# A two-stream hybrid layer on one NeuronCore: the pivots and the last range's statistics in PSUM banks

## Chip, core and metric

The kernel runs on one core of a Trainium2 chip. The metric is the device time of one execution in microseconds (us). The four engines that compute are TensorE (PE; PEld is its weight load), VectorE (DVE), ScalarE (ACT) and GpSimd (POOL). SyncE (SP) issues DMAs. SBUF is the memory that all engines read; TensorE writes its products to banks of PSUM, which VectorE and ScalarE read and write too.

## The reference

One layer of a hybrid encoder is computed for a prompt (1024 frames) and for running streams (32 frames), 1056 columns in all, with the same weights. What matters here are the two residual sublayers at its end, each with a layer norm over the 1024 features:

```python
mix = jnp.concatenate([hm, hf, hg], axis=-1) @ w_o
x = _layer_norm(ALPHA * x + (1 + g1) * mix, ln1_g, ln1_b)
h = x * (1 + sc2) + sh2
y = (jax.nn.silu(h @ w_gate) * (h @ w_up)) @ w_down
x = _layer_norm(ALPHA * x + (1 + g2) * y, ln2_g, ln2_b)
# _layer_norm: mu = mean(x); var = mean((x - mu)^2); (x - mu) * rsqrt(var + eps) * g + b
```

## The kernel before

**Layout.** Features lie on the 128 partitions in eight blocks (`k` or `m`, 0 to 7), frames along the free axis. The frames are two parts, c=0 (512) and c=1 (544), and each is worked in two ranges (256 and 256, 272 and 272; `MM` and `LN`). A large product takes three matmuls per block: the operand and the weight are split into a high and a low part, and hi·hi, hi·lo and lo·hi are added (`gemm`, L131 to L133; the names end in `whi`/`wlo`, `ah`/`al`, `acth`/`actl`). Weights come by DMA, ScalarE casts the high part (L118) and VectorE subtracts for the low one (L119).

**Order of stages.** Projections, the head groups, then `wo0`: the output projection and first layer norm (`lna0`) of c=0. After that heads of the other part, the SwiGLU products of c=0 (`up0`, `dn0`) interleaved with what is left of the attention heads, then `wo1`, `lna1`, `up1`, `dn1` for c=1 with the second layer norm (`lnb`). A tile scheduler fixes each engine's order ahead of the run from a cost model; `issue_after` keeps what follows behind a named instruction, and pools with a fixed number of buffers make a new tile wait for the release of an old one. PSUM has three pools in the late stages: `pg` (3 banks, `"g"`), `pu` (3 banks, `"gu"`) and `pt` (2 banks, `"t"`); while the attention runs `pss` (2 banks, `"s"`) stands in place of `pu`.

**A residual update.** `sublayer_end` (L1185 on) adds one finished block from its PSUM bank to the residual tile `z` on VectorE (L1195, `scalar_tensor_tensor`, STT below). The bank is free for the next product when this is done. So VectorE's queue up to L1195 decides when TensorE may begin the product that reuses the bank.

**The pivot.** To keep the sums of squares small, the column mean of the first finished block is taken off all eight blocks (`ln_pivot`, L1049). A matmul with a matrix of ones (L1052) forms it in a `"t"` bank, ScalarE copies it to SBUF (`pv`, L1053), VectorE subtracts it from the first block (L1054), and GpSimd from each other block (L1189) before that block's L1195.

**The sums.** `ln_sum` squares a block on ScalarE (L1063) into an SBUF tile `tmp` (4 buffers); GpSimd or VectorE adds blocks up to `zs` (L1067, GpSimd in `wo1` and `dn1`) and VectorE the squares to `qs` (L1069). In the last range of all, the last two blocks aren't added but go to the matmul with ones beside `zs` and `qs` (`late`, `rest`, L1079).

**The closing norm.** `ln2` (L1436) forms mean and mean square by matmul, copies the mean to SBUF (L1445), forms the variance (L1446), Ln and Exp on ScalarE, a Newton step on VectorE (L1088 to L1090), then per block: minus mean (L1448, VectorE), times 1/std (L1464, VectorE), gain and offset (L1466 on ScalarE, L1468 on VectorE for the last block), and a store per two blocks, the last two singly (L1471). c=1 does range 272 first (`half` 0), whose norm is woven into the second range's products; range 0 (`half` 1) ends the kernel.

## Time and profile before

| | us |
|---|---|
| median of three timed runs | 1342.64 (1341.70 to 1343.36) |
| the profiled execution's own time | 1339.63 |
| its span in the trace | 1337.8 |
| TensorE busy in the span | 1320.8 (99%) |
| VectorE / ScalarE / GpSimd busy | 990.1 / 651.2 / 212.9 |

A row of the timeline gives the start in us, the duration, the engine, the line, the operation, output<-inputs, shapes and types, and how many instructions in a row were put together (x3); in brackets the idle time of that engine just before, and what ended it. A row of the waits gives an engine and line, what it waited for, the total in us, how often, and the longest. A row of the windows gives, for a stretch, each engine's busy time and instructions, the granted TensorE clock, the DMA share and GB/s. The lines named below are those of the kernel before.

### The profile page before, as it was taken

The numbers are of one execution on the slowest core, as the hardware profiler recorded it, in microseconds if no ns is written. First come the engines' busy times: TensorE is split into PE (matmuls) and PEld (weight loads), VectorE is DVE, ScalarE is ACT, GpSimd is POOL, SyncE is SP. The second block draws the span as 40 slices with busy tenths as digits, with TensorE's granted clock in tenths as the row PEclk, the third lists the DMA queues.
The fourth block names the chain that finished last, engine by engine and source line by source line (L and its number), as shares of the span: only waits on it lengthen the run. The fifth ranks groups of instructions, "written<-read, shape, count | busy, mean of one in ns | idle before, by whom it ended". The sixth has DMA issues, their size and how long they took to land.

```text
span 1337.8 us, 24992 instructions
## 1 busy us (share of the span) xinstructions
PE 1320.8 (99%) x9428; PEld 1198.5 (90%) x9428; DVE 990.1 (74%) x2081; ACT 651.2 (49%) x1291; POOL 212.9 (16%) x242
## 2 busy tenths in 40 slices
...
GB/s 362 280 257 168 174 180 183 148 129 110 234 178 249 172 156 113 132 153 127 118 130 116 88 119 80 228 153 113 208 236 148 227 198 165 195 121 150 87 48 67
DMA packets 118120, 217.43 MB, mean 163 GB/s; under 512 B 18325, under 2 KB 62481, under 8 KB 118001
## 3 DMA queue, kind: packets, MB, share of 16 engines
...
q8 instruction: 74, 1.21, 0.4%
q10 hardware_dynamic: 1200, 0.62, 0.2%
...
## 4 chain that ended last, share of the span: by engine, by line
PE 95%; DVE 2%; DMA 2%; ACT 1%; issue 0%; SPq 0%; DVEq 0%
PE up_g L131 6%; PE up_g L133 6%; PE up_g L132 6%; PE dn_g L131 4%; PE dn_g L132 4%; PE dn_g L133 4%; PE tm_g L405 3%; PE tm_g L407 3%; PE tm_g L406 3%; PE sup_u L133 3%; PE sup_u L132 3%; PE sup_u L131 3%; PE fox_t L939 2%; PE wo_g L131 2%; PE wo_g L133 2%; PE wo_g L132 2%
## 5 line engine op out<-in xcount | busy, mean ns | idle before, releaser
L131 PE MATMUL up_g<-ada_ah,up_whi 128*128 128x512 f32 (+1 forms) x384 | 140.8, 367 | 0.0
L132 PE MATMUL up_g<-ada_al,up_whi 128*128 128x512 f32 (+1 forms) x384 | 140.7, 366 | 0.0
L133 PE MATMUL up_g<-ada_ah,up_wlo 128*128 128x512 f32 (+1 forms) x384 | 139.7, 364 | 0.0
L1364 ACT CAST sup_whi<-sup_raw 128x1024 fp32r<-128x1024 f32 x54 | 56.6, 1050 | 97.6 <-PE dn_u L132 41.3
L912 ACT ACTIVATE fox_p<-fox_s,fox_fmx 128x384 f32<-128x384 f32 (+2 forms) x96 | 55.1, 578 | 59.4 <-DVE fox_fmx L910 39.8
L131 PEld LDWEIGHTS up_g<-ada_ah,up_whi 128*128 128x128 f32 x384 | 72.5, 189 | 11.7 <-issue 0.4
L133 PEld LDWEIGHTS up_g<-ada_ah,up_wlo 128*128 128x128 f32 x384 | 72.6, 189 | 11.2
L132 PEld LDWEIGHTS up_g<-ada_al,up_whi 128*128 128x128 f32 x384 | 72.6, 189 | 10.6
L1365 DVE TENSOR_TENSOR sup_wlo<-sup_raw,sup_whi 128x1024 fp32r<-128x1024 f32 x54 | 69.0, 1279 | 15.1 <-ACT sup_whi L1364 15.1
L1195 DVE SCALAR_TENSOR_TENSOR wo_z<-dn_g,start_mod,wo_z 128x512 f32<-128x512 f32 (+4 forms) x120 | 60.1, 520 | 21.7 <-PE dn_g L133 21.1
L118 ACT CAST up_whi<-up_raw 128x1024 fp32r<-128x1024 f32 x50 | 52.4, 1049 | 47.4 <-PE dn_g L132 19.0
L132 PE MATMUL dn_g<-up_actl,dn_whi 128*128 128x512 f32 (+2 forms) x200 | 73.2, 367 | 0.0
L133 PE MATMUL dn_g<-up_acth,dn_wlo 128*128 128x512 f32 (+2 forms) x200 | 73.2, 366 | 0.0
L131 PE MATMUL dn_g<-up_acth,dn_whi 128*128 128x512 f32 (+2 forms) x200 | 73.1, 366 | 0.0
L119 DVE TENSOR_TENSOR up_wlo<-up_raw,up_whi 128x1024 fp32r<-128x1024 f32 x50 | 63.6, 1272 | 11.3 <-ACT up_whi L118 10.2
L944 ACT CAST fox_pth<-fox_t 128x512 fp32r<-128x512 f32 (+1 forms) x80 | 41.3, 542 | 51.6 <-PE fox_t L939 45.5
L907 DVE TENSOR_REDUCE fox_fmx<-fox_s 128x1 f32<-128x384 f32 (+2 forms) x96 | 53.0, 553 | 15.5 <-PE fox_s L904 14.1
L118 ACT CAST dn_whi<-dn_raw 128x1024 fp32r<-128x1024 f32 (+1 forms) x44 | 42.7, 970 | 43.3 <-PE up_g L132 26.8
L945 DVE TENSOR_TENSOR fox_ptl<-fox_t,fox_pth 128x512 fp32r<-128x512 f32 (+1 forms) x80 | 49.8, 632 | 9.8 <-ACT fox_pth L944 9.6
L119 DVE TENSOR_TENSOR dn_wlo<-dn_raw,dn_whi 128x1024 fp32r<-128x1024 f32 (+1 forms) x44 | 49.5, 1125 | 8.0 <-ACT dn_whi L118 8.0
L1316 POOL DMA_DIRECT2D start_dp<-w_gu x19 | 20.2, 1063 | 212.8 <-DMA start_dp<-w_gu 212.8
L405 PE MATMUL tm_g<-tm_whi,start_ah 128*128 128x264 f32 (+2 forms) x160 | 49.9, 312 | 0.0
...
## 6 DMA issues: line engine op xcount, KB each, us to landing
...
```

The source lines that it names most:

```text
L118: nc.scalar.copy(hi[:, :w], raw[:, :w])
L119: (eng or nc.vector).tensor_tensor(lo[:, :w], raw[:, :w], f(hi[:, :w]), ALU.subtract)
L131: nc.tensor.matmul(ps, hi, xh(k), start=start and k == 0, stop=False)
L132: nc.tensor.matmul(ps, hi, xl(k), start=False, stop=False)
L133: self.lastmm = nc.tensor.matmul(ps, lo, xh(k), start=False, stop=stop and k == n - 1)
L405: nc.tensor.matmul(ps[:, :ncol], xh, hi, start=k == 0, stop=False)
L907: nc.vector.tensor_reduce(mxs[:, x:x + 1], s[:, :w], AX.X, ALU.max, negate=True)
L912: nc.scalar.activation(pr[:, lo:hi], banks[x][:, :hi - lo], AF.Exp, bias=mxs[:, 0:1], accum_out=sums[:, x:x + 1])
L945: nc.vector.tensor_tensor(pl[:, :e], ps[:, :e], f(ph[:, :e]), ALU.subtract)
L1195: self.lastz = self.nc.vector.scalar_tensor_tensor(z[:, m, x:y], ps[:, x - a:y - a], g[i], z[:, m, x:y], ALU.mult, ALU.add)
L1364: nc.scalar.copy(h, x)
L1365: tt(l, x, f(h), ALU.subtract)
```

## The change

Four things are done; c=1's other stages and all matmuls of the products are the same.

1. Where sums are taken (`wo0`, `wo1`), the pivot stays in its PSUM bank. ScalarE's copy goes. VectorE takes the pivot off every block with an STT that reads the bank (`ln_off`, L1061 of the changed kernel), eight times per range; GpSimd's 28 subtractions (L1189) go. In `wo0` the bank is from `pss`, in `wo1` from `pt`.
2. `ln2_half` (c=1, first range): mean and 1/std stay in `pt` banks and VectorE reads them there.
3. `ln_sum` in the last range: squares go to `pg`/`pu` banks (the last one to SBUF), and the addition of a square to `qs` is issued behind the update of the block after it.
4. `ln2_last` (c=1, second range): mean, variance and 1/std in banks; VectorE subtracts the mean from blocks 0 to 2 and GpSimd, from an SBUF copy, from 3 to 7; then VectorE multiplies all eight; blocks 5 and 7 get gain and offset on VectorE, the others on ScalarE. Only the seventh and eighth block's sums and the eighth's square go to the matmul with ones directly.

```diff
     def ln_pivot(self, st, z, sl):
         nc = self.nc
-        ps = self.t(self.pt, [P, 512], F32, "t")
         n = sl.stop - sl.start
+        pool, tag = st["bank"]
+        ps = self.t(pool, [P, 512], F32, tag)
         nc.tensor.matmul(ps[:, :n], self.onesm, z[:, sl], start=True, stop=True)
+        if st["sum"]:
+            st["off"][sl.start] = ps[:, :n]
+            self.ln_off(st, z, sl)
+            return
         nc.scalar.activation(st["pv"][:, sl], ps[:, :n], AF.Copy, scale=float(D // P))
         nc.vector.tensor_tensor(z[:, sl], z[:, sl], st["pv"][:, sl], ALU.subtract)
+
+    def ln_off(self, st, z, sl):
+        self.nc.vector.scalar_tensor_tensor(z[:, sl], st["off"][sl.start], -float(D // P), z[:, sl], ALU.mult, ALU.add)
...
-        sq = self.t(self.p2, [P, 272], F32, "tmp", 4)[:, :sl.stop - sl.start]
+        if st["last"] and m != o[7]:
+            sq = self.t((self.pg, self.pu)[m % 2], [P, 512], F32, self.utag[m % 2])[:, :sl.stop - sl.start]
+        else:
+            sq = self.t(self.p2, [P, 272], F32, "tmp", 4)[:, :sl.stop - sl.start]
         nc.scalar.activation(sq, z[:, m, sl], AF.Square)
+        add = lambda: nc.vector.tensor_tensor(st["qs"][:, sl], st["qs"][:, sl], sq, ALU.add)
+        if st["last"]:
+            with self.tc.issue_after(self.lastz.ins):
+                st["last"].pop()()
+            st["last"].append(add if m != o[7] else None)
+            add = lambda: None
...
         if pivot and not first and st["sum"]:
-            less()
+            self.ln_off(st, z[:, m], sl)
...
+    def ln2_last(self, st, a, b):
+        self.phase = "lnb1"
+        nc, z, sl, n = self.nc, self.z[1], slice(a, b), b - a
+        bank = lambda pool, tag: self.t(pool, [P, 512], F32, tag)[:, :n]
+        pm, pq = bank(self.pt, "t"), bank(self.pt, "t")
+        for p, parts in ((pm, [st["zs"][:, sl]] + [x for x, _ in st["rest"]]), (pq, [st["qs"][:, sl], st["rest"][-1][1]])):
+            for i, y in enumerate(parts):
+                nc.tensor.matmul(p, self.onesm, y, start=i == 0, stop=i == len(parts) - 1)
+        v, r = bank(self.pg, "g"), bank(self.pg, "g")
+        s = self.t(self.p2, [P, 272], F32, "tmp", 4)[:, :n]
+        mean, r0 = st["zs"][:, sl], st["pv"][:, sl]
+        nc.scalar.activation(s, pm, AF.Square)
+        nc.scalar.copy(mean, pm)
+        less = lambda k: nc.vector.tensor_tensor(z[:, k, sl], z[:, k, sl], pm, ALU.subtract)
+        for k in range(2):
+            less(k)
+        first = nc.vector.scalar_tensor_tensor(v, pq, self.epsa, s, ALU.add, ALU.subtract)
+        nc.scalar.activation(r0, v, AF.Ln)
+        nc.scalar.activation(r0, r0, AF.Exp, scale=-0.5)
+        with self.tc.issue_after(first.ins):
+            last = less(2)
+        for k in range(3, KT):
+            nc.gpsimd.tensor_tensor(z[:, k, sl], z[:, k, sl], mean, ALU.subtract)
+        with self.tc.issue_after(last.ins):
+            nc.vector.scalar_tensor_tensor(v, v, -0.5, r0, ALU.mult, ALU.mult)
+            nc.vector.tensor_tensor(v, v, r0, ALU.mult)
+            nc.vector.scalar_tensor_tensor(r, v, 1.5, r0, ALU.add, ALU.mult)
+            for k in range(KT):
+                zk = z[:, k, sl]
+                nc.vector.tensor_tensor(zk, zk, r, ALU.mult)
+                self.ln2_end(k, a, b, nc.scalar if k == 6 else nc.sync, k in (5, 7))
...
+        st["bank"] = (self.pss, "s")
...
             if half:
-                st["late"] = st["order"][6:]
+                st["late"], st["last"] = st["order"][6:], [lambda: None]
...
-            end = self.ln2(1, st, a, b, TAFF[half], True)
             if half:
-                weave(end)
+                self.ln2_last(st, a, b)
             else:
+                end = self.ln2_half(st, a, b)
                 next(end)
```

The scheduler moves instructions beyond these lines. On TensorE everything ahead of `wo0` stands as before; from there to `wo1` the order of attention heads, `up0` and `dn0` among each other differs, and after `wo1` it is the same up to the last range. Three places follow, in each the order before and then the changed one.

In the rows of the changed kernel L1212 is the update (L1195 before), L118 the low part (L119), L130 to L132 the products (L131 to L133), L1074 the sum of squares (L1069), L1083 `zs` (L1067).

VectorE in `wo1`, around the first block's updates (`g` are banks with finished products, two ranges per block: 1855 and 1856 are the first block's, 1862 and 1863 the second's, 1869 and 1870 the third's; `t` are the pivots' banks; `wlo` the low parts of weights). Before:

```order
L1054 TENSOR_TENSOR wo1_z1_1851_9897<-wo1_z1_1851_9897,wo1_pv_1850_9896 128x272
L1195 SCALAR_TENSOR_TENSOR wo1_z1_1851_9897<-wo1_g_1856_9906,start_mod_48_152,wo1_z1_1851_9897 128x240
L1195 SCALAR_TENSOR_TENSOR wo1_z1_1851_9897<-wo1_g_1856_9906,start_mod_48_152,wo1_z1_1851_9897 128x32
L1195 SCALAR_TENSOR_TENSOR wo1_z1_1851_9897<-wo1_g_1862_9975,start_mod_48_152,wo1_z1_1851_9897 128x272
L119 TENSOR_TENSOR wo1_wlo_1882_10182<-wo1_raw_1880_10179,wo1_whi_1881_10181 128x1024
L1069 TENSOR_TENSOR wo1_qs_1849_9895<-wo1_qs_1849_9895,wo1_tmp_1864_10003 128x272
L119 TENSOR_TENSOR wo1_wlo_1889_10252<-wo1_raw_1887_10249,wo1_whi_1888_10251 128x1024
L1054 TENSOR_TENSOR wo1_z1_1851_9897<-wo1_z1_1851_9897,wo1_pv_1850_9896 128x272
L1195 SCALAR_TENSOR_TENSOR wo1_z1_1851_9897<-wo1_g_1869_10045,start_mod_48_152,wo1_z1_1851_9897 128x272
L1195 SCALAR_TENSOR_TENSOR wo1_z1_1851_9897<-wo1_g_1863_9976,start_mod_48_152,wo1_z1_1851_9897 128x240
```

Changed:

```order
L1212 SCALAR_TENSOR_TENSOR wo1_z1_1851_9895<-wo1_g_1855_9903,start_mod_48_152,wo1_z1_1851_9895 128x272
L1212 SCALAR_TENSOR_TENSOR wo1_z1_1851_9895<-wo1_g_1856_9904,start_mod_48_152,wo1_z1_1851_9895 128x240
L1212 SCALAR_TENSOR_TENSOR wo1_z1_1851_9895<-wo1_g_1856_9904,start_mod_48_152,wo1_z1_1851_9895 128x32
L118 TENSOR_TENSOR wo1_wlo_1882_10178<-wo1_raw_1880_10175,wo1_whi_1881_10177 128x1024
L1061 SCALAR_TENSOR_TENSOR wo1_z1_1851_9895<-wo1_t_1857_9954,wo1_z1_1851_9895 128x272 x8
L1061 SCALAR_TENSOR_TENSOR wo1_z1_1851_9895<-wo1_t_1858_9960,wo1_z1_1851_9895 128x272 x3
L1212 SCALAR_TENSOR_TENSOR wo1_z1_1851_9895<-wo1_g_1862_9971,start_mod_48_152,wo1_z1_1851_9895 128x272
L1061 SCALAR_TENSOR_TENSOR wo1_z1_1851_9895<-wo1_t_1858_9960,wo1_z1_1851_9895 128x272 x5
L1212 SCALAR_TENSOR_TENSOR wo1_z1_1851_9895<-wo1_g_1863_9972,start_mod_48_152,wo1_z1_1851_9895 128x240
L1212 SCALAR_TENSOR_TENSOR wo1_z1_1851_9895<-wo1_g_1863_9972,start_mod_48_152,wo1_z1_1851_9895 128x32
```

One low-part subtraction (`wlo_1882`) now stands ahead of the pivots, the other (`wlo_1889`) behind the second block's updates, and sixteen subtractions of the pivots stand among them, three of the second range's ahead of the second block's first update.

TensorE in the first block of `wo1` (`ah0`, `al0` are the operand of range 0, `ah272`, `al272` that of range 272, whose last parts are still being made then). Before:

```order
L132 MATMUL wo1_g_1855_9905<-up0_al0_1830_9828,wo1_whi_1853_9901 128x272
L133 MATMUL wo1_g_1855_9905<-up0_ah0_1828_9826,wo1_wlo_1854_9902 128x272
L131 MATMUL wo1_g_1855_9905<-up0_ah0_1828_9826,wo1_whi_1853_9901 128x272
L132 MATMUL wo1_g_1855_9905<-up0_al0_1830_9828,wo1_whi_1853_9901 128x272
L133 MATMUL wo1_g_1855_9905<-up0_ah0_1828_9826,wo1_wlo_1854_9902 128x272
L131 MATMUL wo1_g_1855_9905<-up0_ah0_1828_9826,wo1_whi_1853_9901 128x272
L132 MATMUL wo1_g_1855_9905<-up0_al0_1830_9828,wo1_whi_1853_9901 128x272
L133 MATMUL wo1_g_1855_9905<-up0_ah0_1828_9826,wo1_wlo_1854_9902 128x272
L131 MATMUL wo1_g_1855_9905<-up0_ah0_1828_9826,wo1_whi_1853_9901 128x272
L132 MATMUL wo1_g_1856_9906<-up0_al272_1831_9829,wo1_whi_1853_9901 128x272
```

Changed:

```order
L132 MATMUL wo1_g_1855_9903<-up0_ah0_1828_9824,wo1_wlo_1854_9900 128x272
L130 MATMUL wo1_g_1856_9904<-up0_ah272_1829_9825,wo1_whi_1853_9899 128x272
L131 MATMUL wo1_g_1856_9904<-up0_al272_1831_9827,wo1_whi_1853_9899 128x272
L132 MATMUL wo1_g_1856_9904<-up0_ah272_1829_9825,wo1_wlo_1854_9900 128x272
L130 MATMUL wo1_g_1855_9903<-up0_ah0_1828_9824,wo1_whi_1853_9899 128x272
L131 MATMUL wo1_g_1855_9903<-up0_al0_1830_9826,wo1_whi_1853_9899 128x272
L132 MATMUL wo1_g_1855_9903<-up0_ah0_1828_9824,wo1_wlo_1854_9900 128x272
```

Before, the range 0 products ran ahead, those of range 272 came in as their operand came; changed, the two ranges take turns block by block, three matmuls each.

VectorE at the end of the kernel, from the seventh block's update on (`dn1_u`, `dn1_g` finished products or, in the changed kernel's L1074, squares; `lnb1_t` matmul sums; `sup_pv`, `sup_zs` SBUF copies). Before:

```order
L1195 SCALAR_TENSOR_TENSOR wo1_z1_1851_9897<-dn1_g_2704_15848,start_mod_48_152,wo1_z1_1851_9897 128x272
L1069 TENSOR_TENSOR sup_qs_2570_14857<-sup_qs_2570_14857,dn1_tmp_2701_15819 128x272
L1069 TENSOR_TENSOR sup_qs_2570_14857<-sup_qs_2570_14857,dn1_tmp_2703_15840 128x272
L1195 SCALAR_TENSOR_TENSOR wo1_z1_1851_9897<-dn1_u_2706_15868,start_mod_48_152,wo1_z1_1851_9897 128x272
L1446 SCALAR_TENSOR_TENSOR lnb1_tmp_2710_15896<-lnb1_t_2709_15892,start_epsa_37_115,lnb1_tmp_2710_15896 128x272
L1448 TENSOR_TENSOR wo1_z1_1851_9897<-wo1_z1_1851_9897,sup_zs_2569_14856 128x272 x3
L1088 SCALAR_TENSOR_TENSOR lnb1_tmp_2710_15896<-lnb1_tmp_2710_15896,sup_pv_2571_14858 128x272
L1089 TENSOR_TENSOR lnb1_tmp_2710_15896<-lnb1_tmp_2710_15896,sup_pv_2571_14858 128x272
L1090 SCALAR_TENSOR_TENSOR sup_pv_2571_14858<-lnb1_tmp_2710_15896,sup_pv_2571_14858 128x272
L1464 TENSOR_TENSOR wo1_z1_1851_9897<-wo1_z1_1851_9897,sup_pv_2571_14858 128x272 x3
L1448 TENSOR_TENSOR wo1_z1_1851_9897<-wo1_z1_1851_9897,sup_zs_2569_14856 128x272
L1464 TENSOR_TENSOR wo1_z1_1851_9897<-wo1_z1_1851_9897,sup_pv_2571_14858 128x272
```

Changed:

```order
L1212 SCALAR_TENSOR_TENSOR wo1_z1_1851_9895<-dn1_g_2705_15843,start_mod_48_152,wo1_z1_1851_9895 128x272
L1074 TENSOR_TENSOR sup_qs_2570_14853<-sup_qs_2570_14853,dn1_u_2704_15835 128x272
L1212 SCALAR_TENSOR_TENSOR wo1_z1_1851_9895<-dn1_u_2707_15864,start_mod_48_152,wo1_z1_1851_9895 128x272
L1074 TENSOR_TENSOR sup_qs_2570_14853<-sup_qs_2570_14853,dn1_g_2706_15857 128x272
L1545 TENSOR_TENSOR wo1_z1_1851_9895<-wo1_z1_1851_9895,lnb1_t_2709_15885 128x272 x2
L1548 SCALAR_TENSOR_TENSOR lnb1_g_2711_15892<-lnb1_t_2710_15886,start_epsa_37_115,lnb1_tmp_2713_15894 128x272
L1545 TENSOR_TENSOR wo1_z1_1851_9895<-wo1_z1_1851_9895,lnb1_t_2709_15885 128x272
L1556 SCALAR_TENSOR_TENSOR lnb1_g_2711_15892<-lnb1_g_2711_15892,sup_pv_2571_14854 128x272
L1557 TENSOR_TENSOR lnb1_g_2711_15892<-lnb1_g_2711_15892,sup_pv_2571_14854 128x272
L1558 SCALAR_TENSOR_TENSOR lnb1_g_2712_15893<-lnb1_g_2711_15892,sup_pv_2571_14854 128x272
L1561 TENSOR_TENSOR wo1_z1_1851_9895<-wo1_z1_1851_9895,lnb1_g_2712_15893 128x272 x8
L1524 TENSOR_SCALAR wo1_z1_1851_9895<-wo1_z1_1851_9895,start_colp_33_107 128x272 x2
```

The last addition to `qs` now stands behind the last update, two of the three first mean subtractions ahead of the variance, the other five are gone from this queue, and the eight multiplications stand in a row with one more gain and offset behind them.

54 lines of the change are left out of this document (44 added, 10 removed).

## Prediction

> **What bounds the kernel now.** I read the page first, for the engine that is busy.
>
> ```profile
> PE 1320.8 (99%) x9428; PEld 1198.5 (90%) x9428; DVE 990.1 (74%) x2081; ACT 651.2 (49%) x1291; POOL 212.9 (16%) x242
> PE 95%; DVE 2%; DMA 2%; ACT 1%; issue 0%; SPq 0%; DVEq 0%
> ```
>
> TensorE is busy for 1320.8 of 1337.8 us and makes 95% of the chain that ended last. The change leaves the products alone, so it can only touch the 17.0 us in which TensorE does nothing. Where these lie, the waits of TensorE say, and the windows of the long stretches between.
>
> ```profile
> PE wo_g L131 <- DVE wo_z L1195: 2.2, 1, 2.2
> PE lnb_t L1079 <- POOL sup_zs L1067: 0.2, 1, 0.2
> ```
>
> ```profile
> 420.00:830.00 410.00, 410.00 (x2291) 343.92 (x2291) 294.59 (x611) 208.67 (x431) 16.48 (x23) 1.00 0.46 129
> 905.00:1322.00 417.00, 417.00 (x3334) 416.21 (x3333) 357.33 (x660) 217.54 (x367) 83.74 (x80) 1.00 0.55 155
> ```
>
> From 420 to 830 and from 905 to 1322 TensorE never stops: nothing is to be won there, only to be lost. Two places are left that the change reaches: one wait of 2.2 us in `wo1`, and the end, from the last product to the last store.
>
> **The wait in wo1.** The timeline there, VectorE (and two updates of the last range, for their price), then GpSimd, then TensorE:
>
> ```profile
> 862.25 5.03 DVE L119 TENSOR_TENSOR wo_wlo<-wo_raw,wo_whi 128x1024 fp32r<-128x1024 f32 x1
> 880.79 1.21 DVE L119 TENSOR_TENSOR wo_wlo<-wo_raw,wo_whi 128x1024 fp32r<-128x1024 f32 x1
> ...
> 1315.05 0.50 DVE L1195 SCALAR_TENSOR_TENSOR wo_z<-dn_g,start_mod,wo_z 128x272 f32<-128x272 f32 x1
> 1315.47 0.49 DVE L1195 SCALAR_TENSOR_TENSOR wo_z<-dn_u,start_mod,wo_z 128x272 f32<-128x272 f32 x1
> ```
>
> ```profile
> 860.52 5.61 POOL L1189 TENSOR_TENSOR wo_z<-wo_z,wo_pv 128x272 f32<-128x272 f32 x7
> 867.87 7.00 POOL L1189 TENSOR_TENSOR wo_z<-wo_z,wo_pv 128x272 f32<-128x272 f32 x7
> ```
>
> ```profile
> 857.84 0.62 PE L1052 MATMUL wo_t<-wo_z,start_onesm 128*128 128x272 f32 x2
> ...
> 868.78 0.28 PE L132 MATMUL wo_g<-up_al,wo_whi 128*128 128x272 f32 x1
> 868.90 0.28 PE L133 MATMUL wo_g<-up_ah,wo_wlo 128*128 128x272 f32 x1
> 871.37 0.39 PE L131 MATMUL wo_g<-up_ah,wo_whi 128*128 128x272 f32 x1 [2.19 <-DVE wo_z L1195]
> ```
>
> A low part that takes 1.21 us took 5.03 while GpSimd took the pivot off seven blocks: VectorE stood still beside GpSimd, and the updates behind it in its queue freed TensorE's bank late.
>
> Changed, GpSimd has none of these 14 subtractions here, and VectorE has 16 instead. Each reads the bank as the update L1195 does, two of which start 0.42 us apart (1315.05 and 1315.47); I take 0.41, as other pairs of them show it. Count from T0, the end of the first block's products. TensorE does a product of 24 matmuls, 0.12 to 0.13 apart (868.78, 868.90), in 3.0 us, and a pivot in less than 0.5 (0.62 for the row, which the next one overlaps). The first pivot stands behind 22 matmuls of the second block, so VectorE's first burst begins near T0 + 3.5 and ends, 8 x 0.41 later, at 6.8; three more subtractions (1.2) and the second block's first update (0.4) make 8.4; five subtractions and two short updates (0.55 together) make 11.0. `pg` has three banks, so TensorE wants the bank of the second block's first product three products after that product began: 3 x 3.0 + 0.9 for two pivots, T0 + 9.9, and the next one at T0 + 12.9. There is 1.5 to 1.9 us to spare, so the wait goes: **-2.2**.
>
> TensorE's order in the first block of `wo1` has changed too. Before, products of range 0 filled the time until range 272's operand was cast; now the ranges take turns. No row shows what that waits; at one end nothing, at the other the nine matmuls of range 0 that stood in a row ahead of one of range 272, 9 x 0.125 = 1.1 us. I take **+0.4**, nearer to nothing, as in the changed order the work ahead of it on TensorE is a little less.
>
> **wo0.** Here the same 16 subtractions arrive on VectorE and TensorE shows no wait. The pivot's matmul, and VectorE from its idle time to the second block's update:
>
> ```profile
> 365.43 0.59 PE L1052 MATMUL wo_t<-wo_z,start_onesm 128*128 128x256 f32 x2
> ```
>
> ```profile
> 368.57 1.23 DVE L119 TENSOR_TENSOR wo_wlo<-wo_raw,wo_whi 128x1024 fp32r<-128x1024 f32 x1 [5.43 <-ACT wo_whi L118]
> 370.60 0.47 DVE L1195 SCALAR_TENSOR_TENSOR wo_z<-wo_g,start_mod,wo_z 128x256 f32<-128x256 f32 x1
> ```
>
> VectorE sat idle for 5.43 us ahead of 368.57, and the pivot's bank is full from 366.1 on; six of the eight subtractions (2.5 us) fit there, the two others (0.8) take the place of L1054 (about 0.9 until 370.60). So the update stays near 370.6: **0**, hidden by that idle time. Without this cover it costs up to 3.3 us a range. The second range has no such hole; its norm ends an estimated 1 to 3 us later (3.3 for the burst, less what the L1054 that goes took), and the last operand that `up0` waits for is made here:
>
> ```profile
> 432.66 0.69 DVE L1242 TENSOR_TENSOR ada_al<-lna_sil,ada_ah 128x512 fp32r<-128x512 f32 x1
> ```
>
> ```profile
> 435.40 0.28 PE L131 MATMUL up_g<-ada_ah,up_whi 128*128 128x256 f32 x1
> ```
>
> It is done at 433.35; the last of the 24 matmuls of the product that reads it start at about 435.4, 2 us later, so the first 2 us of a delay cost nothing. So +0 to +1 here, up to +3 with what else was moved, and I take **+0.4** for this and for the other reordering up to `wo1`, where TensorE had no idle time at all.
>
> **The end, up to the variance.** VectorE, GpSimd, TensorE:
>
> ```profile
> 1310.28 0.44 DVE L1296 TENSOR_TENSOR up_sil<-up_u,up_sil 128x272 f32<-128x272 f32 x1
> 1310.63 0.43 DVE L1089 TENSOR_TENSOR lnb_tmp<-lnb_tmp,sup_pv 128x272 f32<-128x272 f32 x1
> ...
> 1317.04 1.01 DVE L1448 TENSOR_TENSOR wo_z<-wo_z,sup_zs 128x272 f32<-128x272 f32 x1
> ...
> 1323.95 0.50 DVE L1195 SCALAR_TENSOR_TENSOR wo_z<-dn_u,start_mod,wo_z 128x272 f32<-128x272 f32 x1
> ```
>
> ```profile
> 1316.89 0.85 POOL L1067 TENSOR_TENSOR sup_zs<-sup_zs,wo_z 128x272 f32<-128x272 f32 x1
> ```
>
> ```profile
> 1321.99 0.29 PE L133 MATMUL dn_u<-up_acth,up_al 128*128 128x272 f32 x1
> 1322.48 0.73 PE L1079 MATMUL lnb_t<-sup_zs,start_onesm 128*128 128x272 f32 x2 [0.21 <-POOL sup_zs L1067]
> ...
> 1325.11 0.62 PE L1079 MATMUL lnb_t<-wo_z,start_onesm 128*128 128x272 f32 x2
> 1325.57 0.62 PE L1079 MATMUL lnb_t<-dn_tmp,start_onesm 128*128 128x272 f32 x2
> ```
>
> The last product ends at 1322.3, but VectorE begins the last update at 1323.95, because instructions with two SBUF inputs stretch from 0.44 to 1.01 us beside GpSimd's sums. With the mean, 1/std and squares in banks they have one SBUF input. From 1315.05 the changed order has 8 updates and 12 others ahead of the free queue: 8 x 0.41 + 12 x 0.36 = 7.6, so VectorE keeps up, and the last update starts with its product, at about 1322.5 instead of 1323.95. (L1296 reads one operand from a bank and its successor starts 0.35 later, the same as behind an instruction of SBUF alone; that is the 0.36.) The additions to `qs` now wait behind the next block's update; queued behind each are the next update and what is left of the other range's norm, and TensorE waits for the bank of the square that it reads: squares in `pg` and `pu` make its banks scarcer, 0 to 0.4 us, inside the range below.
>
> The matmuls with ones then bind: five instead of six, 0.46 apart (1325.11 to 1325.57), the first from 1322.5 with 0.1 for a wait: 1322.5 + 0.56 + 3 x 0.46 + 0.62 = 1325.1, against 1326.2. So the variance starts 1.1 us earlier: **-1.1** (-0.4 to -1.5).
>
> **The end, from the variance.**
>
> ```profile
> 1326.29 0.50 DVE L1446 SCALAR_TENSOR_TENSOR lnb_tmp<-lnb_t,start_epsa,lnb_tmp 128x272 f32<-128x272 f32 x1 [1.85 <-ACT lnb_tmp L1444]
> ...
> 1329.18 1.15 DVE L1464 TENSOR_TENSOR wo_z<-wo_z,sup_pv 128x272 f32<-128x272 f32 x3
> ...
> 1334.50 0.42 DVE L1468 TENSOR_SCALAR wo_z<-wo_z,start_colp 128x272 f32<-128x272 f32 x1
> ```
>
> ```profile
> 1329.66 2.14 ACT L1466 ACTIVATE wo_z<-wo_z,start_colp 128x272 f32<-128x272 f32 x4 [1.94 <-DVE wo_z L1464]
> ...
> 1334.32 0.35 ACTq L1471 DMA_DIRECT2D o_yT<-wo_z  x1
> ```
>
> ```profile
> 1331.50:1331.75 0.25, 0.00 (x0) 0.00 (x0) 0.21 (x2) 0.25 (x1) 0.00 (x0) 0.50 0.10 30
> 1335.00:1336.25 1.25, 0.00 (x0) 0.00 (x0) 0.00 (x0) 0.00 (x0) 0.00 (x0) 0.50 0.84 281
> 1336.25:1336.50 0.25, 0.00 (x0) 0.00 (x0) 0.00 (x0) 0.00 (x0) 0.00 (x0) 0.50 0.04 9
> ```
>
> The steps from L1446 to the first multiplication (2.9 us) stay. VectorE's work behind it shrinks: before, from 1329.18 to 1334.9 (5.7 us), as five mean subtractions stand between; now 8 multiplications and 2 gains, 10 x 0.36 = 3.6. GpSimd's five subtractions (some 0.85 each, as its sum at 1316.89) start with the mean, some 3 us ahead of the first multiplication, and stay ahead. ScalarE's six gains take 0.53 each (2.14 / 4), 3.2 us. But the output has to leave: eight blocks of 128 x 272 x 4 bytes are 1.11 MB, at 281 GB/s 4.0 us. Before, data began 2.3 us behind the first multiplication (1331.5) and ended at 1336.4. Changed, the first multiplication is at 1328.1, data begin at 1330.4 and end, one after the other, at 1334.4: 2.0 us earlier. Of these 1.1 are counted above, so **-0.9** (-0.5 to -1.4).
>
> VectorE's writes into a bank (variance, 1/std) show in no row; as reads from one cost 0 (L1296) to 0.05 us (L1195's 0.41 apart) I set 0 to 0.3, inside these bounds. [...]
>
> **The sum.** -2.2 + 0.4 + 0.4 - 1.1 - 0.9 = -3.4. On the profiled execution's 1339.6 that is 1336.2. The median of the runs lies 3.0 above that execution, so 1342.6 - 3.4 = **1339.2**. About 0.2% (2.7 us) is what a measurement of this kernel can tell from no change.
>
> **Rivals.**
> 1. *The end is bound elsewhere (0.22).* If the variance waits as before, because TensorE waits for banks that hold squares or VectorE is still late, and the stores queue as before, the end gives 0.8 instead of 2.0: about 1340.4, no change that can be told. For it: ScalarE's gains and the stores were near their limits already. Against: VectorE's 5.7 us lay ahead of the last store.
> 2. *Slower: VectorE becomes late in wo0 (0.08).* The subtractions stand in its queue ahead of the updates that free the banks. If the first burst isn't covered by the idle 5.43 us, it costs 3.3 us, the second range's the same, and if both fall on TensorE that is 6.6: -3.4 + 6.6 = +3.2, 1345.8. It decides from 3.4 us of new waits on. For it: no TensorE idle time is there to absorb it. Against: the pivot's bank is full long before 368.57.
> 3. *GpSimd still holds VectorE up in wo1 (0.10).* Its sums of blocks remain, as do VectorE's low parts with two SBUF inputs; if the bank is freed late again, the 2.2 stays: 1341.4. Against: a single sum is 0.85 us, not seven in a row.
> 4. *All covers hold (0.15).* Neither 0.4 is paid and the end gives 2.9: -5.1, 1337.5.
>
> **How the numbers follow.** The forecast has 0.45, with 1338 to 1340.3 as its own range; three quarters of it lie beyond 2.7 us. Faster: 0.34 + 0.15, and 0.06 of the first rival's, 0.55. Slower: 0.06 of the second. The rest, 0.39, is within. The range goes from the fourth rival, 1337.5, less 0.2, to 1342.8, where the third rival with a further 1.4 us of waits in the reordered middle still lies; the second stays outside.
>
> **What would show it.** Right: no wait of TensorE on VectorE's updates in `wo1`; low parts there at 1.2 us; VectorE's last update about 0.2 us behind the last product; L1446's successor about 2.9 us behind that; 1.1 MB out in about 4 us. Wrong: waits of TensorE in `wo0` or at `up0`'s first blocks, in the first block of `wo1` or between the last products, of more than 1 us in all; a span that shrinks by less than 2 us while the end is as computed.

## The result, and the profile after

| | before | changed |
|---|---|---|
| median of 6 runs each, us | 1342.17 (1339.93 to 1343.36) | 1335.16 (1334.02 to 1335.78) |
| the profiled execution, us | 1339.63 (span 1337.8) | 1335.24 (span 1333.1) |

The ratio of the runs is 0.995 (95% interval 0.9937 to 0.9963): 6.7 us faster (the medians are 7.0 apart). Forecast was 3.4 us and 1339.2, with 1337.3 as the lower end; the time lies below the range. The two profiled executions are only 4.4 us apart (4.7 in the span). So there are two questions: where the 4.4 came from, and why the runs differ by 2.3 us more.

First the page of the changed kernel (busy time, and the chain that ended last), then the waits of TensorE.

```profile
PE 1318.8 (99%) x9426; PEld 1197.1 (90%) x9426; DVE 989.8 (74%) x2106; ACT 648.3 (49%) x1285; POOL 183.0 (14%) x219
PE 96%; DMA 1%; ACT 1%; SPq 0%; DVE 0%; issue 0%; ACTq 0%
```

```profile
PE start_o L294 <- DVE start_onesm L161: 1.2, 1, 1.2
...
PE wo_g L130 <- DVE wo_z L1212: 0.2, 1, 0.2
```

GpSimd has 30 us less to do (183.0 against 212.9), and no wait of TensorE in `wo1` is left. The 0.2 us on an update is in `wo0`. VectorE's queue in the changed kernel, first in `wo0` (the pivots' bank is called `wo_s` there), then in `wo1`:

```profile
365.11 2.08 DVE L1061 SCALAR_TENSOR_TENSOR wo_z<-wo_s,wo_z 128x256 f32<-128x256 f32 x6 [2.92 <-PE wo_s L1052]
368.52 1.23 DVE L118 TENSOR_TENSOR wo_wlo<-wo_raw,wo_whi 128x1024 fp32r<-128x1024 f32 x1 [1.33 <-ACT wo_whi L117]
369.66 0.75 DVE L1061 SCALAR_TENSOR_TENSOR wo_z<-wo_s,wo_z 128x256 f32<-128x256 f32 x2
370.32 0.87 DVE L1212 SCALAR_TENSOR_TENSOR wo_z<-wo_g,start_mod,wo_z 128x256 f32<-128x256 f32 x2
...
859.59 3.92 DVE L1061 SCALAR_TENSOR_TENSOR wo_z<-wo_t,wo_z 128x272 f32<-128x272 f32 x11 [1.04 <-PE wo_t L1052]
863.43 0.49 DVE L1212 SCALAR_TENSOR_TENSOR wo_z<-wo_g,start_mod,wo_z 128x272 f32<-128x272 f32 x1
863.83 1.83 DVE L1061 SCALAR_TENSOR_TENSOR wo_z<-wo_t,wo_z 128x272 f32<-128x272 f32 x5
865.57 0.62 DVE L1212 SCALAR_TENSOR_TENSOR wo_z<-wo_g,start_mod,wo_z 128x240 f32<-128x240 f32 x2
866.10 1.22 DVE L118 TENSOR_TENSOR wo_wlo<-wo_raw,wo_whi 128x1024 fp32r<-128x1024 f32 x1
```

In `wo0` six subtractions fill the idle time and two follow the low part; the update starts at 370.32, where it started at 370.60 before. In `wo1` the update that held TensorE up ends at 866.2, ahead of the low part. That takes 1.22 us (5.03 before); in the second profile of this kernel (after_again) it takes 2.42. GpSimd's sums, which remain, start ahead of it there (865.19) and behind its start here (866.69). The updates are done by then.

The end of the changed kernel: TensorE from the last product, VectorE from the last update, and two windows of the output's DMA.

```profile
1319.46 0.29 PE L132 MATMUL dn_u<-up_acth,up_al 128*128 128x272 f32 x1
1319.59 0.62 PE L1539 MATMUL lnb_t<-sup_zs,start_onesm 128*128 128x272 f32 x2
...
1321.42 0.62 PE L1539 MATMUL lnb_t<-dn_tmp,start_onesm 128*128 128x272 f32 x2
```

```profile
1319.79 0.50 DVE L1212 SCALAR_TENSOR_TENSOR wo_z<-dn_u,start_mod,wo_z 128x272 f32<-128x272 f32 x1 [0.66 <-PE dn_u L132]
...
1321.86 0.79 DVE L1545 TENSOR_TENSOR wo_z<-wo_z,lnb_t 128x272 f32<-128x272 f32 x2 [1.23 <-ACT sup_zs L1544]
1322.57 0.50 DVE L1548 SCALAR_TENSOR_TENSOR lnb_g<-lnb_t,start_epsa,lnb_tmp 128x272 f32<-128x272 f32 x1
...
1325.45 2.87 DVE L1561 TENSOR_TENSOR wo_z<-wo_z,lnb_g 128x272 f32<-128x272 f32 x8
1328.24 0.74 DVE L1524 TENSOR_SCALAR wo_z<-wo_z,start_colp 128x272 f32<-128x272 f32 x2
```

```profile
1325.40:1328.00 2.60, 0.00 (x0) 0.00 (x0) 2.56 (x9) 2.08 (x5) 0.13 (x1) 0.52 0.01 3
1328.00:1331.60 3.60, 0.00 (x0) 0.00 (x0) 0.98 (x3) 1.05 (x3) 0.00 (x0) 0.50 0.94 307
```

The last update starts 0.04 us behind the last product's end (1319.75); before it was 1.7 late. From that product's end to the variance it is 2.82 us (1322.57), before 4.01 (1326.29 less 1322.28): 1.2 gained. From the variance to the span's end it is 10.6 us, before 11.5: 1.0 gained. The last product itself ends 2.5 us earlier; 2.2 of that is the wait in `wo1`. The rest, 0.3, has no single owner: a wait of 0.5 in the heads isn't there, two of 0.4 (a weight's DMA) and 0.2 (in `wo0`) are new, and in a second profile of the changed kernel the last product starts at 1318.95, another 0.5 earlier, so that tenths here are chance. So 2.2 + 0.3 + 1.2 + 1.0 is the trace's 4.7.

### The profile page after: what moved, and what is told of

It reads as the page before. It is cut to its first block, busy times and chain, and to the rows that moved or that the text cites. A ratio compares the mean times of both kernels' runs of the same rounds, so it can differ in the third digit from the quotient of the medians.

```text
span 1333.1 us, 24982 instructions
## 1 busy us (share of the span) xinstructions
PE 1318.8 (99%) x9426; PEld 1197.1 (90%) x9426; DVE 989.8 (74%) x2106; ACT 648.3 (49%) x1285; POOL 183.0 (14%) x219
## 4 chain that ended last, share of the span: by engine, by line
PE 96%; DMA 1%; ACT 1%; SPq 0%; DVE 0%; issue 0%; ACTq 0%
PE up_g L132 6%; PE up_g L130 6%; PE up_g L131 6%; PE dn_g L132 4%; PE dn_g L130 4%; PE dn_g L131 4%; PE tm_g L404 4%; PE tm_g L406 3%; PE tm_g L405 3%; PE sup_u L132 3%; PE sup_u L131 3%; PE sup_u L130 3%; PE fox_t L938 2%; PE wo_g L130 2%; PE wo_g L132 2%; PE wo_g L131 2%
## 5 line engine op out<-in xcount | busy, mean ns | idle before, releaser
L131 PE MATMUL up_g<-ada_al,up_whi 128*128 128x512 f32 (+1 forms) x384 | 140.5, 366 | 0.0
L132 PE MATMUL up_g<-ada_ah,up_wlo 128*128 128x512 f32 (+1 forms) x384 | 140.3, 365 | 0.0
L130 PE MATMUL up_g<-ada_ah,up_whi 128*128 128x512 f32 (+1 forms) x384 | 140.1, 365 | 0.0
L130 PEld LDWEIGHTS up_g<-ada_ah,up_whi 128*128 128x128 f32 x384 | 72.4, 189 | 11.5 <-issue 0.4
L131 PEld LDWEIGHTS up_g<-ada_al,up_whi 128*128 128x128 f32 x384 | 72.4, 189 | 11.0
L132 PEld LDWEIGHTS up_g<-ada_ah,up_wlo 128*128 128x128 f32 x384 | 72.5, 189 | 10.7
L1212 DVE SCALAR_TENSOR_TENSOR wo_z<-dn_g,start_mod,wo_z 128x512 f32<-128x512 f32 (+4 forms) x120 | 60.2, 521 | 22.7 <-PE dn_g L132 22.3
L130 PE MATMUL dn_g<-up_acth,dn_whi 128*128 128x512 f32 (+2 forms) x200 | 73.7, 370 | 0.0
L132 PE MATMUL dn_g<-up_acth,dn_wlo 128*128 128x512 f32 (+2 forms) x200 | 73.7, 368 | 0.0
L131 PE MATMUL dn_g<-up_actl,dn_whi 128*128 128x512 f32 (+2 forms) x200 | 73.4, 368 | 0.0
L118 DVE TENSOR_TENSOR up_wlo<-up_raw,up_whi 128x1024 fp32r<-128x1024 f32 x50 | 64.6, 1293 | 8.6 <-ACT up_whi L117 7.7
L118 DVE TENSOR_TENSOR dn_wlo<-dn_raw,dn_whi 128x1024 fp32r<-128x1024 f32 (+1 forms) x44 | 49.5, 1126 | 9.8 <-ACT dn_whi L117 9.7
```

The source lines that it names most:

```text
L118: (eng or nc.vector).tensor_tensor(lo[:, :w], raw[:, :w], f(hi[:, :w]), ALU.subtract)
L130: nc.tensor.matmul(ps, hi, xh(k), start=start and k == 0, stop=False)
L131: nc.tensor.matmul(ps, hi, xl(k), start=False, stop=False)
L132: self.lastmm = nc.tensor.matmul(ps, lo, xh(k), start=False, stop=stop and k == n - 1)
L1212: self.lastz = self.nc.vector.scalar_tensor_tensor(z[:, m, x:y], ps[:, x - a:y - a], g[i], z[:, m, x:y], ALU.mult, ALU.add)
```

## The experiments

Unless another is named, the kernel of comparison is the one before, run beside the others on the same chip: 1340.04 (27 runs) for the first four kernels, 1340.91 (34) for the next four, 1342.28 (12) for the last four.

### Each half alone, and both kernels again

**before_again** and **after_again** are the two kernels, unedited.

> The kernel before, unchanged, for a second profile. Its six timed executions so far lie at 1339.9 to 1340.0 (two) and 1341.7 to 1343.4 (four); its trace shows one of the low ones. Theory A (the upper group pays 2 to 3 us more at the pivots, where VectorE and GpSimd meet) and theory B (it pays them at the end of the kernel): both groups again, and a trace of the upper group would show its 2 to 3 us there. Theory C (executions differ by this whatever the kernel): the kernels of this set show two groups as well.

Measured: 1341.61 (1338.47 to 1343.08, 11 runs).

> The changed kernel, unchanged, beside the others on one chip: 7 us below the kernel before by theories A and B, in one group; theory C: sometimes only 4.5 us below.

Measured: 1335.49 (1334.76 to 1337.11, 6 runs), ratio 0.9969 (0.9958 to 0.9981).

**pivot_only** is the kernel before with the first of the four points of the change alone:

```diff
+        if st["sum"]:
+            st["off"][sl.start] = ps[:, :n]
+            self.ln_off(st, z, sl)
+            return
...
-            less()
+            self.ln_off(st, z[:, m], sl)
```

> Only the pivots as in the change (bank, VectorE instead of GpSimd); the end as before. By the two traces the products end 2.5 us earlier and nothing else moves: 2.5 us below the kernel before's trace. Theory A: median 4.5 to 5.5 us below the kernel before, one group. Theory B and C: 2 to 3 us below.

Measured: 1336.67 (1335.71 to 1339.59, 11 runs), ratio 0.9979 (0.9970 to 0.9988). No wait in `wo1`.

**tail_only** is the changed kernel with these lines undone, so that only points 2 to 4 are left.

> Only the last ranges' statistics as in the change; the pivots as before, with the 2.2 us wait of TensorE in wo1. By the two traces the end is 2.2 us shorter. Theory A: median 2 to 2.5 us below, still two groups. Theory B: 4.5 to 5 us below, one group. Theory C: 2 to 2.5 us below, two groups as in every kernel.

Measured: 1339.34 (1337.10 to 1341.14, 11 runs), ratio 0.9993 (0.9983 to 1.0002). Five runs lie at 1337.1 to 1337.7, six at 1339.3 to 1341.1. TensorE's wait in `wo1` is back with 2.7 us.

The medians of three kernels missed what was expected. By the ratios after_again gains 4.2 us where 7 was expected, pivot_only 2.8 (theory A had 4.5 to 5.5) and tail_only 0.9 (2 to 2.5). All three numbers took the median of the kernel before as known, about 1342. Beside these kernels it was 1340.04, as 15 of the 27 runs lay in the lower group; so the gain in the median hangs on how many runs of the kernel before fall in the upper one. These medians don't choose between the theories.

The run that explained the rest was before_again's profile. Its execution took 1342.74 us, the span is 1340.9, which is 3.1 more than in the profile on which the forecast was built, for the same program. Here are TensorE's timeline at the wait, and four windows of 3.41 us there.

```profile
868.68 0.28 PE L133 MATMUL wo_g<-up_ah,wo_wlo 128*128 128x272 f32 x1
871.62 0.59 PE L131 MATMUL wo_g<-up_ah,wo_whi 128*128 128x272 f32 x1 [2.66 <-DVE wo_z L1195]
872.02 0.43 PE L132 MATMUL wo_g<-up_al,wo_whi 128*128 128x272 f32 x1
872.24 0.43 PE L133 MATMUL wo_g<-up_ah,wo_wlo 128*128 128x272 f32 x1
872.47 0.43 PE L131 MATMUL wo_g<-up_ah,wo_whi 128*128 128x272 f32 x1
```

```profile
867.53:870.95 3.42, 1.44 (x12) 1.22 (x10) 3.42 (x4) 0.00 (x0) 3.42 (x4) 1.00 0.80 107
870.95:874.36 3.41, 2.73 (x12) 2.74 (x13) 2.85 (x6) 2.12 (x4) 3.41 (x5) 0.50 1.02 330
874.36:877.77 3.41, 3.41 (x17) 3.41 (x17) 3.03 (x6) 0.43 (x1) 3.41 (x4) 0.50 0.62 200
877.77:881.19 3.42, 3.42 (x29) 3.42 (x29) 2.66 (x4) 1.08 (x2) 2.46 (x3) 1.00 0.78 173
```

The third column from the right is the granted clock; 1.00 is the full one. It is 0.50 for 6.8 us, from 870.95, two us into the wait of 2.66, to 877.77. For the 6.2 us behind the wait the matmuls are 0.23 us apart instead of 0.125: some 27 of them at 0.1 us more each, 2.7 us lost *behind* the wait, while TensorE counts as busy. With 0.5 for the longer wait this is about the 3.1. In the profile of the forecast the wait was 2.19 and the clock stayed at 1.00:

```profile
866.52:869.93 3.41, 2.66 (x22) 2.45 (x20) 3.41 (x4) 0.00 (x0) 3.41 (x4) 1.00 0.57 63
869.93:873.35 3.42, 1.98 (x15) 1.98 (x16) 2.86 (x7) 1.84 (x4) 3.42 (x5) 1.00 1.02 272
```

These windows are chosen with a reason. In all fourteen profiles the granted clock changes only at points that lie a whole multiple of 3.413 us apart (the stretch at 1.00 lasts 1324.37 us, 388 times 3.4133, in the profile of the forecast, and 1320.96 us, 387 times 3.4133, in the changed kernel's); each window runs from one such point to the next. In the whole record the clock fell behind every window in which TensorE idled for 1.98 us or more, and behind none with 1.72 or less; it came back behind windows with at most 0.15 idle, and not behind those with 0.68 or more. So in these traces it isn't the length of the wait alone that decides, but how much of it falls into one window. In before_again 1.98 us did (3.42 less the 1.44 in which TensorE was busy). In the profile of the forecast a point at 869.93 parted the wait into 0.75 and 1.44, and nothing happened. This was read from the traces afterwards; no run was made that moves a wait against these points.

The runs without a profile agree. One or two windows of 3.41 us at half clock lower the mean granted clock of a run of 1340 by 0.001 or 0.003. Of the 84 executions of the kernel before in this section, 35 have a mean clock of 0.997 or more and average 1339.5 us; 49 have less and average 1341.9. With three decimals the mark is coarse, and the two groups overlap (1338.8 to 1341.6). Of the changed kernel's 12, eleven have 0.997 or more. So the changed kernel loses a wait, and with it a clock loss of about 2.4 us that some six in ten executions paid. The points fit that share: a wait of 2.2 to 2.7 us that begins anywhere between two of them leaves less than 1.85 us in either window in three to four cases of ten, by estimate from the two bounds above (35 of 84 are four in ten). A trace and a correlation are not yet a proof; the next four kernels fill the wait, or put one in.

### Does the wait lower the clock?

**before_busy** is the kernel before with twenty matmuls, whose result nobody reads, put into the wait in `wo1`. Its blocks wait as long as before, but TensorE doesn't idle.

```diff
+                if c == 1 and m == 3 and a == 0:
+                    spare = self.t(self.pt, [P, 512], F32, "t")[:, :b - a]
+                    for _ in range(20):
+                        nc.tensor.matmul(spare, w[0][0], hh[a][:, ko[0], :b - a], start=True, stop=True)
```

> The kernel before with 20 idle matmuls (into a bank nobody reads, 0.125 us each, 2.5 us) between the third and fourth block's products of wo1, where TensorE waits 2.2 to 2.7 us. Theory (after a wait of this length the granted clock falls to 0.50 for some 5 us in most executions, which costs 2 to 3 us more): the clock stays at 1.00 there, all executions lie in the lower group, 1338.5 to 1340.5, median 1 to 2 us below the kernel before. Rival (the upper group comes from elsewhere): both groups as before, median as before or up to 0.5 us above.

Measured: 1339.99 (1338.73 to 1341.25, 12 runs), ratio 0.9993 (0.9984 to 1.0003). The twenty matmuls and the windows around them:

```profile
869.15 2.69 PE L1163 MATMUL wo_t<-up_ah,wo_whi 128*128 128x272 f32 x20
```

```profile
872.00:874.00 2.00, 2.00 (x17) 2.00 (x18) 1.44 (x4) 1.56 (x3) 2.00 (x4) 1.00 0.96 362
874.00:876.00 2.00, 2.00 (x19) 2.00 (x18) 2.00 (x4) 0.56 (x2) 2.00 (x3) 1.00 0.97 385
```

The clock holds at 1.00, and all 12 runs have a mean clock of 0.997 or 0.998; of the 34 runs of the kernel before beside them 14 have. The upper times are gone: 15 of those 34 lie above 1341.25, none of these 12. By its median the gain is 0.9 us, a little less than the 1 to 2 that were expected, and the ratio's interval alone doesn't part it from 1; the clocks do. The idle work itself costs little: the 12 average 0.6 us above the 14 that kept their clock.

**hold3, hold6, hold9** go the other way: the changed kernel with a wait put back where the old one was. One idle matmul, three, six or nine copies on ScalarE, and one more idle matmul stand ahead of the product.

```diff
+                    with self.tc.issue_after(self.lastmm.ins):
+                        d = nc.tensor.matmul(spare, w[0][0], hh[a][:, ko[0], :b - a], start=True, stop=True)
+                    nc.scalar.copy(x, spare)
+                    for _ in range(2):        # 5 in hold6, 8 in hold9
+                        nc.scalar.copy(x, x)
+                    with self.tc.issue_after(d.ins):
+                        d = nc.tensor.matmul(spare, self.onesm, x, start=True, stop=True)
```

> The changed kernel with TensorE held up at the same place by a chain: one idle matmul, three copies on ScalarE, one more idle matmul that reads them. A wait of about 1.6 us plus 0.6 us for the two matmuls. Both theories: 2.0 to 2.5 us above the changed kernel, clock 1.00 there.

> The same with six copies: a wait of about 3.0 us plus 0.6. Theory: the clock falls to 0.50 for some 5 us in most executions, 6 us above the changed kernel (3.6 + 2.5), some at 3.6. Rival (a wait costs what it lasts): 3.6 us above, clock 1.00.

> The same with nine copies: a wait of about 4.4 us plus 0.6. Theory: the clock falls in every execution, 7.5 us above the changed kernel (5.0 + 2.5) or somewhat more. Rival: 5.0 us above, clock 1.00.

| | wait in the trace | clock at or behind it | median | above after_again |
|---|---|---|---|---|
| hold3 | 3.6 | 0.50 for 6.8 us | 1340.50 (1339.22 to 1343.69, 12) | 5.0 |
| hold6 | 4.7 | 0.50 for 3.4 us | 1342.89 (1340.91 to 1345.72, 12) | 7.4 |
| hold9 | 6.4 | 0.50 for 6.8 us | 1343.84 (1342.70 to 1346.38, 12) | 8.4 |

The control failed in one respect: ScalarE had other work in its queue (a cast and two squares, from 869.89 to 871.49), so hold3's wait came out at 3.6 us instead of the 1.6 that was meant. The waits of hold6 and hold9 are longer than meant too (3.0 and 4.4). The full clock that was expected of hold3 can't be tested by it, and no run has a short wait put in. What the three show is that each wait costs more than itself, by 1.4, 2.7 and 2.0 us (the last column less the first; up to 0.6 of it may be the two idle matmuls, by the estimate ahead of the runs, and after_again wasn't measured beside them). Hold3's wait and its windows follow. The wait is put down to VectorE's low part, which ended 0.01 us behind the last copy on ScalarE; in hold6 and hold9 the copy is named.

```profile
PE wo_t L1187 <- DVE wo_wlo L118: 3.6, 1, 3.6
```

```profile
872.00:874.00 2.00, 1.20 (x3) 0.96 (x4) 1.11 (x2) 0.72 (x2) 0.00 (x0) 0.50 1.00 369
874.00:876.00 2.00, 2.00 (x11) 2.00 (x10) 0.00 (x0) 0.00 (x0) 0.59 (x1) 0.50 0.92 243
```

GpSimd has no subtractions in `wo1` here and is nearly idle in these windows (busy for 0.00 and 0.59 of 2.00 us), so the half clock here comes from TensorE's pause and not from GpSimd's subtractions.

### Is it the bank, or GpSimd's absence?

**pivot_wo1** changes the pivots in `wo1` alone (in `wo0` the copy and GpSimd as before):

```diff
+        if st["sum"] and st["eng"] is nc.gpsimd:
...
-            less()
+            if c:
+                self.ln_off(st, z[:, m], sl)
+            else:
+                less()
```

> The kernel before with the pivot in the bank and on VectorE in wo1 alone; wo0 as before, so that the order of the middle stays as before. Theory (the pivots' whole gain is the wait in wo1 and the slow clock behind it): as pivot_only, 1336 to 1337, one group, no wait of TensorE at that place. Rival (the reordered middle or wo0 carries part of it): more than 0.7 us away from pivot_only.

Measured: 1337.94 (1336.88 to 1338.83, 5 runs), ratio 0.9968 (0.9956 to 0.9981). The wait in `wo1` is gone. By median it is 1.3 us above pivot_only, more than the 0.7 that the rival had named; but the two were measured on different chips, and the kernel before lay 2.2 us higher beside this one. The ratios can't settle it either, since they hang on how many runs of the kernel before lost clock. The traces say more. From the first product of `wo1` to the end of the last product it is 469.9 us, in pivot_only 469.3, in the kernel before 472.2 with its clock kept. From the pivot in `wo0` to the first product of `wo1` it is 485.5, in pivot_only 484.6; but the two profiles of the changed kernel differ there as much (485.7 and 484.6). So the gain lies in `wo1`, and a share of `wo0` or of the middle can't be told from chance.

**pivot_sbuf** is the changed kernel with ScalarE's copy of the pivot put back; VectorE subtracts from SBUF, and GpSimd takes no part in the subtractions.

```diff
-        if st["sum"]:
-            st["off"][sl.start] = ps[:, :n]
-            self.ln_off(st, z, sl)
-            return
...
-            self.ln_off(st, z[:, m], sl)
+            self.nc.vector.tensor_tensor(z[:, m, sl], z[:, m, sl], st["pv"][:, sl], ALU.subtract)
```

> The changed kernel, but ScalarE copies the pivot to SBUF and VectorE subtracts it from there: the engine as in the change, the bank not. Theory (GpSimd's run of seven is what held VectorE): within 0.7 us of the changed kernel, no long low part in wo1. Rival (reading the bank is what counts): subtractions of 0.8 us and more beside GpSimd's sums, TensorE waits 1 to 3 us in wo1 again.

Measured: 1338.99 (1336.97 to 1341.12, 8 runs), ratio 0.9977 (0.9964 to 0.9990). That is 3.5 us above after_again, where at most 0.7 was expected. In `wo1` no wait came back: there, taking the work off GpSimd is what counts. But its profile has a wait of 1.1 us in `wo0`. ScalarE, then VectorE there:

```profile
367.99 1.05 ACT L117 CAST wo_whi<-wo_raw 128x1024 fp32r<-128x1024 f32 x1 [6.95 <-DMA wo_raw<-w_o]
368.95 0.38 ACT L1053 ACTIVATE wo_pv<-wo_s 128x256 f32<-128x256 f32 x1
```

```profile
369.08 1.23 DVE L118 TENSOR_TENSOR wo_wlo<-wo_raw,wo_whi 128x1024 fp32r<-128x1024 f32 x1 [5.25 <-ACT wo_whi L117]
370.22 0.42 DVE L1054 TENSOR_TENSOR wo_z<-wo_z,wo_pv 128x256 f32<-128x256 f32 x1
370.56 2.43 DVE L1205 TENSOR_TENSOR wo_z<-wo_z,wo_pv 128x256 f32<-128x256 f32 x7
372.91 0.87 DVE L1208 SCALAR_TENSOR_TENSOR wo_z<-wo_g,start_mod,wo_z 128x256 f32<-128x256 f32 x2
```

The copy stands in ScalarE's queue behind a cast that waited 6.95 us for a weight, so VectorE's idle 5.25 us pass unused and the update starts at 372.91 instead of 370.32. This is the cover whose loss the second rival had priced (3.3 us a range): gone, it cost 1.1. In this profile the bank is worth something in `wo0`, because it takes ScalarE out of the way.

The same profile has a second place, in neither kernel's forecast:

```profile
433.19 1.08 PE L202 MATMUL ada_t<-ada_late,start_c 128*32 128x256 f32 x8 [2.20 <-DMA ada_late<-w_ada]
```

```profile
429.69:433.11 3.42, 1.30 (x14) 0.67 (x13) 3.33 (x8) 3.40 (x8) 3.17 (x4) 1.00 0.90 287
433.11:436.52 3.41, 3.33 (x27) 1.60 (x28) 2.74 (x6) 1.06 (x4) 2.19 (x2) 0.50 0.59 191
```

Here 2.20 us of waiting, for a DMA, was followed by half the clock for one window of 3.41 us: 2.12 of it lay in the window that ended at 433.11, where in the profile of the forecast 2.19 were parted. It is one profile, of the slowest of eight runs (1341.12); what made the other three above 1340 late is open, and whether the edit caused this wait too.

### The two parts of the end

**no_last** takes point 3 away: the squares go to SBUF, their additions aren't delayed, and six matmuls with ones instead of five close the sums.

```diff
-                st["late"], st["last"] = st["order"][6:], [lambda: None]
+                st["late"] = st["order"][6:]
```

> The changed kernel without its part on the squares: they go to SBUF tiles and are added as they come, and the last two go to the matmul with ones (six of these matmuls instead of five). Theory (the squares' banks and their late additions are worth the distance between VectorE's last update and the last product): the variance comes 0.5 to 1.2 us later than in the changed kernel, the rest is the same. Rival (the matmuls with ones bind anyway): 0.46 us later, one matmul.

Measured: 1335.12 (1334.28 to 1335.51, 5 runs), ratio 0.9946 (0.9934 to 0.9959): not slower than the changed kernel. VectorE:

```profile
1320.10 0.50 DVE L1212 SCALAR_TENSOR_TENSOR wo_z<-dn_u,start_mod,wo_z 128x272 f32<-128x272 f32 x1
1322.63 0.51 DVE L1548 SCALAR_TENSOR_TENSOR lnb_g<-lnb_t,start_epsa,lnb_tmp 128x272 f32<-128x272 f32 x1 [2.03 <-ACT lnb_tmp L1543]
1323.05 1.12 DVE L1545 TENSOR_TENSOR wo_z<-wo_z,lnb_t 128x272 f32<-128x272 f32 x3
...
1325.53 2.87 DVE L1561 TENSOR_TENSOR wo_z<-wo_z,lnb_g 128x272 f32<-128x272 f32 x8
```

Its last product starts at 1319.48, as the changed kernel's (1319.46). The last update is 0.3 us later, the variance 0.06, the first multiplication 0.08. Both numbers that were expected missed: the sixth matmul costs its 0.46 us, but in the changed kernel two mean subtractions (0.71 us) stand ahead of the variance instead, and here all three fit behind it, while ScalarE forms Ln and Exp. Banks for the squares were worth nothing that can be measured (the changed kernel itself wasn't measured beside it).

**less_dve** lets VectorE take the mean off all eight blocks, and GpSimd none:

```diff
-        for k in range(3, KT):
-            nc.gpsimd.tensor_tensor(z[:, k, sl], z[:, k, sl], mean, ALU.subtract)
...
+                if k >= 3:
+                    less(k)
```

> The changed kernel with all eight mean subtractions of the last range on VectorE, none on GpSimd; five more stand between the variance and the Newton step. Theory (VectorE's queue sets the end): 5 x 0.35 less the 0.6 us that it waited for Exp, 1.0 to 1.3 us later. Rival (the stores set the end): less than 0.4 us later.

Measured: 1336.25 (1335.55 to 1339.48, 5 runs), ratio 0.9962 (0.9948 to 0.9977).

```profile
1321.82 0.50 DVE L1548 SCALAR_TENSOR_TENSOR lnb_g<-lnb_t,start_epsa,lnb_tmp 128x272 f32<-128x272 f32 x1
1322.23 2.16 DVE L1545 TENSOR_TENSOR wo_z<-wo_z,lnb_t 128x272 f32<-128x272 f32 x6
...
1325.76 2.87 DVE L1561 TENSOR_TENSOR wo_z<-wo_z,lnb_g 128x272 f32<-128x272 f32 x8
```

From the variance to the first multiplication it is 3.94 us, 1.06 more than in the changed kernel (2.88), and the median is 1.1 above no_last's, measured beside it; both are as expected. So GpSimd's share of the subtractions is worth as much as the 1.0 us that the part behind the variance gained. What puts the last update in time, the rest of the gain, wasn't taken out alone. No_last rules out the squares; the mean and 1/std of the first range in banks (point 2) are left, and the rows fit: multiplications and mean subtractions that took up to 1.01 us beside GpSimd's sums (1317.04 in the kernel before) take 0.43 to 0.44 in the changed kernel.

## Why the prediction missed, step by step

- **The wait in wo1 goes (-2.2):** right, and for the reason given. It is gone in pivot_only, and back in tail_only. The update ends at 866.2, ahead of TensorE's need. Only the sign "low parts there at 1.2 us" held by chance: 1.22 in one profile, 2.42 in the other.
- **The reordered first block of wo1 (+0.4) and the middle (+0.4):** neither was paid. From 830 to 905 TensorE never stops now; in the middle its profile has 0.4 us for a weight's DMA, but the second profile of the changed kernel has none, and pivot_wo1, with the order of before there, has 0.4 too.

```profile
830.00:905.00 75.00, 75.00 (x568) 72.99 (x567) 55.15 (x96) 28.32 (x54) 20.53 (x21) 1.00 0.64 179
```

- **wo0 (0):** right, six subtractions in the hole and two behind it, as forecast. TensorE waits 0.2 there. Pivot_sbuf shows what happens when the cover is gone.
- **Up to the variance (-1.1):** measured -1.2. The last update is in time, as forecast. That banks for the squares and a saved matmul bring it isn't so: no_last, without both, has it too (1322.63 against 1322.57). The mean and 1/std in banks remain as the likely reason, which no run takes out alone.
- **From the variance (-0.9):** measured -1.0. Data leave from 1328.0 (forecast 2.3 us behind the first multiplication; measured 2.55), but faster, 307 instead of 281 GB/s.
- **The base:** this is the step that failed. "The median of the runs lies 3.0 above that execution, so 1342.6 - 3.4" took the 3.0 us as a constant that both kernels carry. For the most part it was a cost of the very wait that the change removes, which the term -2.2 priced at its length alone. In the traces the clock fell to 0.50 where TensorE idled for 1.98 us or more of one window of 3.41 us, and in before_again TensorE lost 2.7 us more behind the wait while it counted as busy. The profiled execution had escaped; by the clocks of the runs, some 49 of 84 pay, 2.4 us on average. That the base was 3.0 and not less is chance: all three timed runs lay in the upper group, and in later sets the median of the kernel before was 1340.0 to 1342.3. The changed kernel's median (1335.16) and its profiled execution (1335.24) are 0.1 apart. Of the 4.0 us between 1339.2 and 1335.2, this is 3.0; the unpaid 0.8 and 0.2 more at the end make up the rest.
- **The rivals:** the fourth (all covers hold, -5.1) is nearest to the trace's -4.7, and it too was put on the wrong base. No sign of the first. Of the third, a low part still took 2.42 us beside GpSimd's sums in after_again, but behind the updates, so that no bank is freed late. The second needed 3.4 us of new waits; 0.2 came.

That something was amiss with the base could be read in what was at hand: the profiled execution lay 2.1 us below the fastest of the three timed runs. A profile that is faster than all the runs that it stands for doesn't show what they lose, and the loss was to be looked for at the only pause of TensorE above 1 us between the start and the end. The reason itself came only with the second profile.

The halves nearly add up, if one looks at runs with the clock kept: the kernel before 1339.5 (35 runs); tail_only's lower five 1337.1 to 1337.7, which is 2.2 less (1.2 + 1.0 in the trace); pivot_only 1336.67, 2.8 less. Both together would be 1334.5; the changed kernel had 1335.16 and 1335.49. The difference of 0.7 to 1.0 is not settled by any run, and these runs come from different sets. Nor is it shown why three of pivot_only's eleven runs lie at 1338 to 1339.6.
